# A Griffin / RWKV-7 trunk: half of the FFN's gate and up blocks by seven products of halves

## The chip, the cores and the metric

The kernel runs on one core of a Trainium2 chip. The metric is the time of one execution on the device in microseconds; the median of three runs before the change is 1319.34 us (1317.73 to 1319.41).

## What is computed

The input is 512 tokens of 1024 features, float32. Two layers follow each other: an RG-LRU block and an FFN, then an RWKV-7 block and an FFN, then a norm. The change touches the FFN, which each layer has once:

```python
def _conv_ffn(x, norm, w_up, conv_w, conv_b, w_down):
    h = _rmsnorm(x, norm)
    u = jnp.einsum('btd,df->btf', h, w_up)
    gate = _causal_dwconv(u[..., :D_FF], conv_w, conv_b)
    hid = jax.nn.gelu(gate, approximate=True) * u[..., D_FF:]
    return jnp.einsum('btf,fd->btd', hid, w_down)
```

D_FF is 3072, the convolution has three taps along the tokens, and `x + _conv_ffn(x)` goes on to the next block.

## The kernel before

Activations lie transposed: features on the 128 partitions, the 512 tokens along a row. x is eight such blocks (KB = 8). Every product of float32 is made of three matmuls on float32r parts (`mm3`, lines 51 to 53): high x high, high x low, low x high. So a block of a weight matrix (128 x 128) costs three matmuls of 512 columns. Weights come from HBM as raw tiles of 128 x 1024 floats (512 KB), on SP's queue, in the order of a written plan (`plan_weights`); ACT rounds each to its high part (line 90), DVE subtracts for the low part (line 93). Raw tiles and parts share one ring of 21 slots of 4 KB a partition (`b4`) with the eight pairs of parts of the normed input (`xs`), which stay in it as long as gate and up products need them.

An FFN has 24 gate blocks and 24 up blocks of 128 features. `gate_up` makes a third of them: four gate blocks, four up blocks, and again. `project` takes four blocks at once, over raw tiles of two blocks of the sum by four blocks of output, with four PSUM banks of eight. The norm's root isn't in xs: it comes as a row `rb` that multiplies each result (lines 581 and 592) and is itself made while the first matmuls run (`norm_end`: a sum over partitions on PE, a power on POOL at line 307, a broadcast on PE, a copy on ACT). A gate block then goes through the convolution (ACT line 584, DVE line 586 twice) and the gelu (ACT line 588); an up block is multiplied by rb and by the gelu (lines 592 and 593) and split into parts `hid`. `down` takes a third of the hidden blocks (eight) through w_down and adds to x (line 637) in the first FFN; in the second it works with hid as the stationary operand, so that the result stands by tokens, and adds to `xtok` (line 630), which `by_tokens` has made from x by transposes. The order is: third 0, third 1, down 0, third 2, down 1, down 2.

The framework that builds the queues of the engines keeps roughly to the order of the program, moves instructions by its own planned times, gives out the slots and sets the waits; on the chip each queue runs in order. Weights are asked for three tiles and split two tiles ahead of their use (`next_weights`). Work of other stages is handed out in small steps between the matmuls (`push`, `background`).

Before the first FFN `fin` (line 532) makes x and its parts while the last product of the RG-LRU block runs; before the second the one at line 1444 does so. After the first FFN, `spill` makes the parts for the RWKV-7 block, in tiles that the FFN no longer needs; at the end `finish` (line 1485 on) squares, norms and stores the output.

## Time and profile before

| | us |
|---|---|
| median of three runs | 1319.34 |
| profiled execution, its own time | 1318.34 |
| its span | 1316.6 |
| PE busy | 1296.2 (98%) |
| PE's weight loads busy | 1057.5 (80%) |
| DVE busy | 842.1 (64%) |
| ACT busy | 609.2 (46%) |
| POOL busy | 72.5 (6%) |
| mean granted clock of PE | 0.998 |

Shares are of the span. PE's matmuls overlap one another in the record, so that a matmul's duration there is longer than the distance to the next one's start. In rows that group instructions stand the line, the engine, the operation, the output and inputs with their shapes, how often, and then the total busy time in us and the mean of one in ns; behind the second bar is the idle time of the engine before them and what ended it. Rows of the timeline begin with the start and the duration in us.

### The profile page before, as it was taken

The page shows a single profiled execution, that of the slowest core. Times are in us where ns is not written, and L with a number is a line of the kernel's source. Part 1 is how long each engine was busy: PE and PEld are TensorE (multiplying, and loading weights), DVE is VectorE, ACT ScalarE, POOL GpSimd, SP SyncE. Part 2 cuts the span into 40 slices and gives each one's busy share as a digit, 9 for nine tenths or more (in the row PEclk, how much of TensorE's full clock was granted, in tenths as well). Part 3 has the DMA queues.
Part 4 walks back from the last instruction along what each step waited for, and adds up shares of the span by engine and source line. Part 5 has one row for each costly group of instructions (what it writes and reads, how often), then busy time and mean ns, then how long its engine had stood idle before and what let it go on. Part 6 is the DMA issues. An engine that isn't in the chain of part 4 may idle for free.

```text
span 1316.6 us, 20618 instructions
## 1 busy us (share of the span) xinstructions
PE 1296.2 (98%) x8547; PEld 1057.5 (80%) x8547; DVE 842.1 (64%) x1276; ACT 609.2 (46%) x964; POOL 72.5 (6%) x114
## 2 busy tenths in 40 slices
PE   9999999999999999999999999999999999999998
PEld 7877888888888888876678787778888888888886
DVE  5988756555436555587989975777564554365523
ACT  6897544233224423358844567655542332244311
POOL 4000000000000000021001121210000000000000
PEclk9999999999999999999999999999999999999999
DMA  6323333323233443213303112133333222334311
GB/s 194 116 64 97 96 112 96 96 64 96 97 96 96 128 116 109 95 37 95 108 25 97 43 53 83 43 97 96 97 96 96 64 96 96 96 96 128 113 63 64
DMA packets 72126, 120.30 MB, mean 91 GB/s; under 512 B 9498, under 2 KB 21476, under 8 KB 71904
## 3 DMA queue, kind: packets, MB, share of 16 engines
q1 hardware_dynamic: 70672, 117.20, 28.6%
q8 instruction: 67, 1.10, 0.3%
q10 hardware_dynamic: 576, 1.05, 0.2%
q0 software_dynamic: 784, 0.74, 0.2%
q14 instruction: 27, 0.22, 0.1%
HBM read 114.44 MB, written 4.52 MB: 90 GB/s over the span
## 4 chain that ended last, share of the span: by engine, by line
PE 85%; DVE 8%; ACT 5%; issue 1%; DMA 0%; SPq 0%; POOLq 0%; POOL 0%; DVEq 0%; ACTq 0%
PE acc L51 22%; PE acc L53 22%; PE acc L52 21%; PE acc L626 3%; PE acc L625 3%; PE acc L627 3%; DVE X L1053 1%; DVE wl L93 1%; DVE DA L1051 1%; PE s L1171 1%; ACT L483 1%; PE pd L1253 1%; ACT L472 0%; PE py L1264 0%; PE pe L1215 0%
## 5 line engine op out<-in xcount | busy, mean ns | idle before, releaser
L51 PE MATMUL acc<-xs,wh 128*128 128x512 f32 x896 | 350.2, 392 | 0.3 <-ACT wh L90 0.3
L53 PE MATMUL acc<-xs,wl 128*128 128x512 f32 x896 | 348.3, 390 | 1.4 <-DVE wl L93 1.4
L93 DVE TENSOR_TENSOR wl<-raw,wh 128x1024 fp32r<-128x1024 f32 (+1 forms) x201 | 242.8, 1216 | 166.1 <-PE acc L52 94.8
L52 PE MATMUL acc<-xs,wh 128*128 128x512 f32 x896 | 348.8, 389 | 0.0
L90 ACT CAST wh<-raw 128x1024 fp32r<-128x1024 f32 (+1 forms) x201 | 207.9, 1045 | 259.2 <-DVE wl L93 169.8
L53 PEld LDWEIGHTS acc<-xs,wl 128*128 128x128 f32 x896 | 168.2, 188 | 37.7 <-DVE wl L93 2.2
L51 PEld LDWEIGHTS acc<-xs,wh 128*128 128x128 f32 x896 | 168.1, 188 | 35.4 <-ACT wh L90 0.8
L52 PEld LDWEIGHTS acc<-xs,wh 128*128 128x128 f32 x896 | 168.3, 188 | 34.4
L586 DVE SCALAR_TENSOR_TENSOR cv<-gpad,pv,cv 128x512 f32<-128x512 f32 x96 | 71.9, 749 | 22.1 <-ACT cv L584 21.0
L90 ACT CAST hid<-un 128x512 fp32r<-128x512 f32 x48 | 29.8, 620 | 108.6 <-DVE un L593 108.6
L626 PE MATMUL acc<-wh,hid 128*128 128x512 f32 (+1 forms) x200 | 76.8, 384 | 0.0
L625 PE MATMUL acc<-wh,hid 128*128 128x512 f32 (+1 forms) x200 | 76.5, 382 | 0.0
L627 PE MATMUL acc<-wl,hid 128*128 128x512 f32 (+1 forms) x200 | 75.9, 380 | 0.0
L52 PE MATMUL acc<-hid,wh 128*128 128x512 f32 x192 | 75.7, 394 | 0.0
L53 PE MATMUL acc<-hid,wl 128*128 128x512 f32 x192 | 75.6, 394 | 0.0
L51 PE MATMUL acc<-hid,wh 128*128 128x512 f32 x192 | 75.5, 393 | 0.0
L592 DVE TENSOR_TENSOR un<-acc,rb 128x512 f32<-128x512 f32 x48 | 33.1, 689 | 44.3 <-PE acc L53 44.3
L93 DVE TENSOR_TENSOR hid<-un,hid 128x512 fp32r<-128x512 f32 x48 | 33.2, 691 | 31.1 <-ACT hid L90 31.1
L584 ACT ACTIVATE cv<-gpad,pv 128x512 f32<-128x512 f32 x48 | 39.2, 817 | 20.7 <-DVE gpad L581 20.5
L588 ACT ACTIVATE ge<-cv 128x512 f32<-128x512 f32 x48 | 30.1, 627 | 35.9 <-DVE cv L586 35.9
L630 DVE TENSOR_TENSOR xtok<-xtok,acc 128x512 f32<-128x512 f32 (+1 forms) x25 | 16.6, 666 | 45.5 <-PE acc L627 45.5
L625 PEld LDWEIGHTS acc<-wh,hid 128*128 128x128 f32 x200 | 37.5, 188 | 8.0
(424 smaller groups left out, 2165.8 us busy)
## 6 DMA issues: line engine op xcount, KB each, us to landing
raw<-in_ffn_w_up_dram SPq DMA_DIRECT2D x96, 512.0 KB, 3.8
raw<-in_ffn_w_down_dram SPq DMA_DIRECT2D x48, 512.0 KB, 3.7
raw<-in_rwkv_w_rkv_dram SPq DMA_DIRECT2D x24, 512.0 KB, 3.9
raw<-in_lru_w_in_dram SPq DMA_DIRECT2D x16, 512.0 KB, 3.9
raw<-in_lru_w_out_dram SPq DMA_DIRECT2D x8, 512.0 KB, 3.9
raw<-in_rwkv_w_out_dram SPq DMA_DIRECT2D x8, 512.0 KB, 3.6
xd<-x SPq DMA_DIRECT2D x8, 256.0 KB, 2.0
AR<-xd SPq DMA_DIRECT2D x1, 2048.0 KB, 7.9
```

Of the source, the lines that this page charges most:

```text
L51: nc.tensor.matmul(ps, wh, xh, start=start, stop=False)
L52: nc.tensor.matmul(ps, wh, xl, start=False, stop=False)
L53: nc.tensor.matmul(ps, wl, xh, start=False, stop=stop)
L90: put = (self.nc.vector.tensor_copy if dve else self.nc.scalar.copy)(hi, src)
L93: self.nc.vector.tensor_tensor(lo, src, hi.bitcast(F32), ALU.subtract)
L584: nc.scalar.activation(cv, gp[:, 0:T], AF.Identity, bias=self.vec(f"ffn_conv_b{l}", fb), scale=cw(0))
L586: nc.vector.scalar_tensor_tensor(cv, gp[:, j : j + T], cw(j), cv, ALU.mult, ALU.add)
L588: nc.scalar.activation(ges[o], cv, AF.Gelu_apprx_tanh)
L592: nc.vector.tensor_tensor(un, ps, rbs[0], ALU.mult)
L625: nc.tensor.matmul(ps, hh[:, s], wh[:, k, m], start=kk == 0, stop=False)
L626: nc.tensor.matmul(ps, hl[:, s], wh[:, k, m], start=False, stop=False)
L627: nc.tensor.matmul(ps, hh[:, s], wl[:, k, m], start=False, stop=kk == 7)
```

## The change

The gate and up blocks are taken in twelve pairs an FFN: two gate and two up blocks of the same features. Even pairs (`Whole`) are made as before, but in four products of half a sum each (G0, U0, G1, U1; the digit is the half of the eight blocks of the sum), every product 24 matmuls of 512 columns. Odd pairs (`Halves`) are made by Winograd's form of Strassen's scheme. The two output halves are up and gate, the two halves of the sum are blocks 0 to 3 and 4 to 7, and the columns are halved into tokens 0 to 255 and 256 to 511; seven products of halves take the place of eight. A product is 24 matmuls of 256 columns. Its weight operand is one of four raw tiles or one of three further sums of them, which POOL makes (four additions, one of them in place), split into parts like a raw tile; its moving operand is a half of xs or one of four sums of halves, which `operands` makes once an FFN on DVE and ACT and keeps as parts in tiles named xt. Products 1, 6, 7 and 4 add up in one bank, 5 and 3 in a second, 2 stands alone; ACT copies the first bank away after 1, 6 and 7, and DVE combines the copies with the other banks.

The products of all pairs stand in one list (`seq`); weights are split two products ahead of the one being emitted (`ahead`), and the first pairs overlap in it (one product of pair 2 lies between the fifth and sixth of pair 1). `down` comes after the odd pairs, for four hidden blocks at a time and eight at the end, and the last two products of a Halves pair are issued within it. Its additions to x or xtok double. In the second FFN the up results aren't multiplied by rb any more; the root is a third operand of the additions to xtok. The hidden tiles of half the pairs take x's place there, and the tiles for the RWKV-7 block's parts and the load of the last norm's gain vector (a DMA on POOL's queue) take the place of the sums xt. The raw tiles of the gate and up weights have four blocks of the sum by 256 columns instead of two by 512.

```diff
@@ -108,23 +110,26 @@
-            def dd(third):
+            def gu(six):
+                for i in range(2):
+                    c = six * 512 + i * 256
+                    self.quads.append(len(plan))
+                    for half, r in ((i, 0), (1 - i, 0), (0, 512), (1, 512)):
+                        add(up, r, half * DFF + c, 4, True)
+            def dd(row, n):
                 for g in range(2):
-                    for k in range(0, 8, 2):
-                        add(dn, third * 1024 + k * P, g * 512)
+                    for k in range(0, n, 2):
+                        add(dn, row + k * P, g * 512)
             gu(0)
-            gu(1)
-            dd(0)
-            gu(2)
-            dd(1)
-            dd(2)
+            for six in range(1, 6):
+                gu(six)
+                if six < 5:
+                    dd((six - 1) * 512, 4)
+            dd(2048, 8)
...
+    def norm_part(self, b, gain):
+        hi, lo = self.norm_block(b, gain)
+        if b >= KB // 2:
+            return hi, lo
+        nc, xb, H = self.nc, self.x[:, b, :], T // 2
+        if b % 2 == 0:
+            self.halves = self.b4(F32, (2, 2, H), f"xd{b}")
+        d = self.halves[:, b % 2]
+        nc.scalar.mul(d[:, 0], xb[:, H:], gain)
+        nc.vector.scalar_tensor_tensor(d[:, 1], xb[:, 0:H], gain, d[:, 0], ALU.mult, ALU.subtract)
+        return hi, lo, d[:, 0], d[:, 1]
...
-            def gate_up(third):
-                hid = []
...
-                            hh, hl = hx[:, 0], hx[:, 1]
-                        self.split(un, hh, hl)
...
+            H = T // 2
+            two = lambda ps: ps.rearrange("p (e t) -> p e t", e=2)
+            sums = [pool.tile([P, 2, 4, H], F32R, tag="xt", name="xt", bufs=4) for _ in range(4)]
+            gain = lambda b: self.vec("ffn_norm", l * 8 + b)
+            def operands():
+                n1, t2, t3, t4 = sums
+                def parts(t, k, f):
+                    nc.scalar.copy(t[:, 0, k], f)
+                    nc.vector.tensor_tensor(t[:, 1, k], f, t[:, 0, k].bitcast(F32), ALU.subtract)
+                for k in range(4):
+                    parts(n1, k, xs[k][3])
+                stt, f = nc.vector.scalar_tensor_tensor, {}
+                for k in range(4):
+                    xb = self.x[:, 4 + k, :]
+                    f[k] = two(t("s", 7))
+                    t2f, t4f = f[k][:, 0], f[k][:, 1]
+                    stt(t2f, xb[:, H:], gain(4 + k), xs[k][3], ALU.mult, ALU.add)
+                    parts(t2, k, t2f)
+                    stt(t4f, xb[:, 0:H], gain(4 + k), t2f, ALU.mult, ALU.subtract)
+                for k in range(4):
+                    if k % 2 == 0:
+                        t3f = two(t("s", 7))
+                    stt(t3f[:, k % 2], self.x[:, 4 + k, H:], gain(4 + k), xs[k][2], ALU.mult, ALU.subtract)
+                    parts(t3, k, t3f[:, k % 2])
+                for k in range(4):
+                    parts(t4, k, f[k][:, 1])
+                op = {i: [tuple(part[:, h] for part in xs[k + k0][:2]) for k in range(4)]
+                      for i, k0, h in ((1, 0, slice(0, H)), (2, 4, slice(0, H)), (3, 4, slice(H, T)))}
+                for i, v in ((5, n1), (6, t2), (7, t3), (4, t4)):
+                    op[i] = [(v[:, 0, k], v[:, 1, k]) for k in range(4)]
+                return op
+            op = {}
...
+            rb = lambda u, v: rbs[0][:, u:v].unsqueeze(1).to_broadcast([P, 2, v - u])
+            tt, gt = nc.vector.tensor_tensor, nc.gpsimd.tensor_tensor
+            class Pair:
+                def __init__(pair, n):
+                    i = quads[n]
+                    self.weights_load(i + 4)
+                    pair.n, pair.gp = n, gpads[n % 2]
+                    raws = [self.loaded.pop(i + j) for j in range(4)]
+                    pair.f = dict(zip(pair.names, raws))
+                    pair.w, pair.bank, pair.s = {}, {}, {}
+                def parts(pair, p):
+                    f = pair.f[p]
+                    hi, lo = self.b4(F32R, (4, 256), f"hi{p}"), self.b4(F32R, (4, 256), f"lo{p}")
+                    nc.scalar.copy(hi, f)
+                    tt(lo, f, hi.bitcast(F32), ALU.subtract)
+                    pair.w[p] = hi, lo
...
+            class Whole(Pair):
+                names = ("G0", "U0", "G1", "U1")
+                order = (names,)
+                def weights(pair, p):
+                    pair.parts(p)
+                def product(pair, p):
+                    hi, lo = pair.w.pop(p)
+                    k0 = int(p[1]) * 4
+                    for e in range(2):
+                        if not k0:
+                            pair.bank[p[0], e] = self.bank("acc" + p[0])
+                        ps = pair.bank[p[0], e]
+                        for k in range(4):
+                            c = slice(e * P, e * P + P)
+                            self.mm3(ps, (hi[:, k, c], lo[:, k, c]), xs[k0 + k][:2], k0 + k == 0, k0 + k == 7)
+                        if p == "G1":
+                            tt(pair.gp[:, e, 2:], ps, rbs[0], ALU.mult)
+                            pair.gate(e)
+                        if p == "U1":
+                            if not e:
+                                pair.room()
+                            un = t("s", 7)
+                            tt(un, ps, pair.ge[:, e] if last else rbs[0], ALU.mult)
+                            if not last:
+                                tt(un, un, pair.ge[:, e], ALU.mult)
+                            self.split(un, pair.hid[:, e, 0], pair.hid[:, e, 1])
+                        self.background(1)
+            class Halves(Pair):
+                names = (1, 7, 4, 2)
+                order = ((1, 5, 6, 2, 7), (4, 3))
+                def weights(pair, p):
+                    f = pair.f
+                    if p == 1:
+                        f[5], f[6], f[3] = (self.b4(F32, (4, 256), name) for name in ("S1", "S2", "S4"))
+                        gt(f[5], f[7], f[4], ALU.add)
+                        gt(f[6], f[5], f[1], ALU.subtract)
+                        gt(f[7], f[1], f[7], ALU.subtract)
+                        gt(f[3], f[6], f[2], ALU.subtract)
+                    pair.parts(p)
+                def product(pair, p):
+                    name = {1: "A", 5: "F", 2: "D"}.get(p)
+                    if name:
+                        pair.bank[name] = two(self.bank("acc" + name))
+                    ps = pair.bank[name or {3: "F"}.get(p, "A")]
+                    hi, lo = pair.w.pop(p)
+                    for e in range(2):
+                        c = slice(e * P, e * P + P)
+                        for k in range(4):
+                            self.mm3(ps[:, e], (hi[:, k, c], lo[:, k, c]), op[p][k], bool(name) and e + k == 0, e + k == 4, more=not name)
+                        self.background(0.5)
+                    s, bank, gp = pair.s, pair.bank, pair.gp
+                    lo, hi = slice(0, H), slice(H, T)
+                    if p in (1, 6, 7):
+                        s[p] = two(t("s", 7))
+                        nc.scalar.copy(s[p], bank["A"])
+                    if p == 2:
+                        tt(s[1], s[1], bank["D"], ALU.add)
+                        if not last:
+                            tt(s[1], s[1], rb(0, H), ALU.mult)
+                    if p == 7:
+                        tt(s[7], s[7], bank["F"], ALU.subtract)
+                        tt(gp[:, :, 2 + H :], s[7], rb(H, T), ALU.mult)
+                    if p == 4:
+                        tt(gp[:, :, 2 : 2 + H], bank["A"], rb(0, H), ALU.mult)
+                        for e in range(2):
+                            pair.gate(e)
+                    if p == 3:
+                        tt(s[6], s[6], bank["F"], ALU.subtract)
+                        if not last:
+                            tt(s[6], s[6], rb(H, T), ALU.mult)
+                        pair.room()
+                        for x, h in ((s[1], lo), (s[6], hi)):
+                            tt(x, x, pair.ge[:, :, h], ALU.mult)
+                            nc.scalar.copy(pair.hid[:, :, 0, h], x)
+                            tt(pair.hid[:, :, 1, h], x, pair.hid[:, :, 0, h].bitcast(F32), ALU.subtract)
+            quads = self.quads[l * 12 : l * 12 + 12]
+            pairs, hids = {}, []
+            W, S = Whole.names, Halves.order
+            seq = [(0, p) for p in W] + [(1, p) for p in S[0]] + [(2, W[0])] + [(1, p) for p in S[1]] + [(2, p) for p in W[1:]]
+            for n in range(3, 12, 2):
+                seq += [(n, p) for p in S[0] + S[1]]
+                if n < 11:
+                    seq += [(n + 1, p) for p in W]
+            made, at = [0], [0]
+            def ahead(j):
+                while made[0] < min(j, len(seq)):
+                    n, p = seq[made[0]]
+                    if n not in pairs:
+                        pairs[n] = (Halves if n % 2 else Whole)(n)
+                    pairs[n].weights(p)
+                    made[0] += 1
+            def products(upto, more=2):
+                while True:
+                    n, p = seq[at[0]]
+                    at[0] += 1
+                    ahead(at[0] + more)
+                    pairs[n].product(p)
+                    if p in ("G0", 1):
+                        self.weights_load(quads[n] + (8 if n + 1 < 12 and quads[n + 1] == quads[n] + 4 else 6))
+                    if n == 0 and p in ("G0", "U0"):
+                        start(int(p == "U0"))
+                        if p == "U0":
+                            op.update(operands())
+                    if p == 7:
+                        self.weights_split(quads[n] + 6)
+                    if (n, p) == upto:
+                        return
+            def down(n, b0, blocks, between, then):
+                final = n == 11
+                pieces = blocks // 2
                 for g in range(2):
                     if last:
                         pss = [self.bank(f"acc{o}") for o in range(4)]
                         end = final and g == 1
-                        for cs in [range(4)] if end else [(0,), (1,), (2, 3)]:
+                        for cs in [range(pieces)] if g else [(i,) for i in range(pieces)]:
...
-                                    if cs[-1] == 3:
-                                        n = slice(g * 512 + m.start, g * 512 + m.stop)
-                                        nc.vector.tensor_tensor(xtok[:, b, n], xtok[:, b, n], ps, ALU.add)
+                                            nc.tensor.matmul(ps, hh[:, s], wl[:, k, m], start=False, stop=kk == blocks - 1)
+                                    if cs[-1] == pieces - 1:
+                                        m = slice(g * 512 + m.start, g * 512 + m.stop)
+                                        nc.vector.scalar_tensor_tensor(xtok[:, b, m], ps, self.rs[:, b : b + 1], xtok[:, b, m], ALU.mult, ALU.add)
                                         if final:
-                                            finish(b, n, xtok[:, b, :], pool)
+                                            finish(b, m, xtok[:, b, :], pool)
+                            if not g and cs[0] == 0:
+                                between()
+                        if not g:
+                            then()
...
+            rooms = []
+            def room(b):
+                if b % 2 == 0:
+                    rooms.append(pool.tile([P, 2, 2, T], F32R, tag="xt", name="hx", bufs=4))
+                return rooms[-1][:, b % 2, 0], rooms[-1][:, b % 2, 1]
+            for n in range(3, 12, 2):
+                products((n, 7))
+                if n == 11 and not last:
+                    self.norm_begin()
+                    self.push(self.lora_weights())
+                down(n, 2 * n - 6, 4 if n < 11 else 8, lambda: products((n, 3)), lambda: ahead(at[0] + 2))
             if not last:
                 after()
...
             nc.vector.tensor_tensor(self.x[:, b, :], xr[:, b, :], ps, ALU.add)
-            xs[b] = self.norm_block(b, self.vec("ffn_norm", 8 + b))
+            xs[b] = self.norm_part(b, self.vec("ffn_norm", 8 + b))
...
+        def spill(b, room):
             nc.sync.dma_start(self.xd[:, b, :], self.x[:, b, :])
-            if b < 4:
-                w = t("hid", 12, F32R, 2 * T)
-                room = w[:, 0:T], w[:, T:]
-            else:
-                tag, n = (("ge", 5), ("ge", 5), ("cv", 2), ("un", 2))[b - 4]
-                room = t(tag, n, F32R), t(tag, n, F32R)
-            hs.append(self.norm_block(b, self.vec("rwkv_norm", b), room))
+            hs.append(self.norm_block(b, self.vec("rwkv_norm", b), room(b)))
         self.ffn(0, xs, spill, lambda: self.rwkv_lora(hs))
...
             if not fgs:
-                fgs.append(pool.tile([P, D], F32, name="fg"))
+                fgs.append(pool.tile([P, 2, D], F32, tag="xt", name="fg", bufs=4)[:, 0])
```

More of the change, by code (lines that the diff above doesn't have):

```diff
@@ L547, in ffn @@
             rbs, norm = [], []
-            gpads = [pool.tile([P, T + 2], F32, name=f"gpad{i}") for i in range(2)]
+            gpads = [pool.tile([P, 2, T + 2], F32, name=f"gpad{i}") for i in range(2)]
             for u in gpads:
-                nc.vector.memset(u[:, 0:2], 0.0)
+                nc.vector.memset(u[:, :, 0:2], 0.0)
+            late = []
             xtok = None
@@ new lines, in ffn, with hidden @@
+            op = {}
+            def hidden(n):
+                if last and n // 2 % 2:
+                    if n == 2:
+                        self.drain()
+                    if n % 2 == 0:
+                        self.xhid = self.const.tile([P, 2, 2, 2, T], F32R, tag="x", name="hid", bufs=1)
+                    return self.xhid[:, n % 2]
+                return pool.tile([P, 2, 2, T], F32R, tag="hid", name="hid", bufs=2 if last else 4)
+            rb = lambda u, v: rbs[0][:, u:v].unsqueeze(1).to_broadcast([P, 2, v - u])
```

104 lines of the change are left out of this document (44 added, 60 removed).

## Prediction

> **What bounds the kernel now.** I read the profile's page first (span, busy shares, chain), then the stages, then the rows of single matmuls.
>
> ```profile
> span 1316.6 us, 20618 instructions
> PE 1296.2 (98%) x8547; PEld 1057.5 (80%) x8547; DVE 842.1 (64%) x1276; ACT 609.2 (46%) x964; POOL 72.5 (6%) x114
> PE 85%; DVE 8%; ACT 5%; issue 1%; DMA 0%; SPq 0%; POOLq 0%; POOL 0%; DVEq 0%; ACTq 0%
> ...
> 100.00:158.50 58.50, 58.18 (x256) 47.52 (x255) 45.12 (x60) 34.82 (x49) 0.00 (x0) 1.00 0.29 91
> 180.00:400.00 220.00, 220.00 (x966) 180.98 (x965) 116.58 (x145) 72.64 (x88) 0.00 (x0) 1.00 0.29 91
> 950.00:1200.00 250.00, 250.00 (x1102) 206.68 (x1102) 134.23 (x167) 83.42 (x101) 0.00 (x0) 1.00 0.29 91
> ```
>
> The last three rows are stages: length, then busy time of PE, PEld, DVE, ACT and POOL, granted clock, DMA share, GB/s. Inside both FFNs PE is busy for the whole stage at clock 1.00 while DVE is busy 53% of it (116.58 of 220; 134.23 of 250), ACT 33%, DMA 29%. So an FFN lasts as long as its matmuls, at the rate at which they start. PE's busy time overlaps itself, so the rate comes from start times, in the timeline:
>
> ```profile
> 199.74 0.39 PE L52 MATMUL acc<-xs,wh 128*128 128x512 f32 x1
> ...
> 205.86 0.39 PE L52 MATMUL acc<-xs,wh 128*128 128x512 f32 x1
> ...
> 550.39 0.39 PE L51 MATMUL acc<-hid,wh 128*128 128x512 f32 x1
> ...
> 555.06 0.39 PE L53 MATMUL acc<-hid,wl 128*128 128x512 f32 x1
> ...
> 777.57 0.28 PE L1001 MATMUL acc<-wl,mix 128*128 128x256 f32 x1
> ...
> 779.96 0.28 PE L1000 MATMUL acc<-wh,mix 128*128 128x256 f32 x1
> ...
> 1304.50 0.28 PE L625 MATMUL acc<-wh,hid 128*128 128x256 f32 x1
> ...
> 1310.04 0.28 PE L627 MATMUL acc<-wl,hid 128*128 128x256 f32 x1
> ```
>
> There are 27 starts from the first of these rows to the second: 6.12 / 27 = 226.7 ns for 512 columns with xs as moving operand. The next pair spans 20 starts: 4.67 / 20 = 233.5 ns when the moving operand is hid, a tile of the FFN's own pool. For 256 columns: 2.39 / 20 = 119.5 ns in the v projection, 5.54 / 47 = 117.9 ns in the last product. The page's 0.28 and 0.39 us are latencies and not the price.
>
> **PE's gain.** A pair (two gate and two up blocks) takes 4 blocks x 8 k x 3 parts = 96 matmuls of 512: 96 x 0.2267 = 21.76 us. As halves it takes 7 products x 2 x 4 x 3 = 168 of 256 columns. Two halves cost more than one whole (2 x 117.9 = 235.8 against 226.7), so the eighth that is saved in columns, 2.7 us, isn't all kept. No row shows a 256-column matmul on the tiles named xt, in the FFN's pool, where four products (5, 6, 7, 4) have their moving operand; the other three read xs. Bounds: 117.9 for all seven gives 168 x 0.1179 = 19.81 us, a gain of 1.96 a pair; hid's whole excess of 6.8 ns on the four gives (3 x 117.9 + 4 x 124.7) / 7 = 121.8, or 20.46 us and 1.30 a pair. I take half the excess, since a matmul of half the length is nearer to half of it: (3 x 117.9 + 4 x 121.3) / 7 = 119.8 ns, beside the v projection's 119.5: 20.13 us, 1.63 a pair. Twelve pairs: **19.6 us less** (15.6 to 23.5). Against it, in the first FFN four hidden blocks that lay in the b4 ring move to the FFN's pool, and their 4 x 8 x 3 = 96 matmuls with them to the slower 233.5: +0.7.
>
> [...]
>
> **What DVE and ACT get for it.** Prices by form:
>
> ```profile
> L93 DVE TENSOR_TENSOR wl<-raw,wh 128x1024 fp32r<-128x1024 f32 x199 | 241.5, 1221 | 165.1 <-PE acc L52 94.8 <-ACT wh L90 47.5 <-PE acc L626 14.0
> L586 DVE SCALAR_TENSOR_TENSOR cv<-gpad,pv,cv 128x512 f32<-128x512 f32 x96 | 71.9, 749 | 22.1 <-ACT cv L584 21.0
> L592 DVE TENSOR_TENSOR un<-acc,rb 128x512 f32<-128x512 f32 x48 | 33.1, 689 | 44.3 <-PE acc L53 44.3
> L630 DVE TENSOR_TENSOR xtok<-xtok,acc 128x512 f32<-128x512 f32 x23 | 15.8, 687 | 45.1 <-PE acc L627 45.1
> L90 ACT CAST wh<-raw 128x1024 fp32r<-128x1024 f32 x199 | 206.8, 1049 | 258.1 <-DVE wl L93 169.8 <-DMA raw<-in_ffn_w_down_dram 30.9 <-PE acc L52 17.1
> L1133 ACT COPY x<-acc 128x512 f32<-128x512 f32 x8 | 4.7, 586 | 2.1 <-PE acc L1001 2.0
> L364 ACT ACTIVATE sqin<-xin 128x256 f32<-128x256 f32 x16 | 6.4, 421 | 0.0
> 1310.35 0.42 DVE L630 TENSOR_TENSOR xtok<-xtok,acc 128x256 f32<-128x256 f32 x1 [0.42 <-PE acc L627]
> ```
>
> A whole pair keeps four weight splits (4 x 1.22), gate work (2 x (0.69 + 2 x 0.75)) and up work (2 x 3 x 0.69): 13.4 us of DVE. A halves pair has seven splits (8.5), about nine 512-wide combinations (6.2, and 1.4 more for the root in the first FFN) and the convolution (3.0): 19.1. A sixth down has four splits and eight additions: 4.9 + 5.5 = 10.4. One round of halves, whole and sixth: 42.9 us of DVE in 20.1 + 21.8 + 21.8 = 63.7 us of PE, 67% instead of 53%; ACT similarly 26 us. Both fit on average. The doubled additions of the sixths (16 x 0.69 = 11 us an FFN) lie under matmuls; with that cover gone they would cost up to 11 an FFN. The last root moved into the additions takes 24 multiplications of 0.69 off DVE in the second FFN and turns each token addition into a three-operand one (0.75 beside 0.69): on the path only at the very end, +0.03 us. Both are off PE: 0.
>
> **The weight sums on POOL.** Four 128x1024 additions a halves pair, 48 in all. POOL has no such row; the nearest:
>
> ```profile
> L1285 POOL TENSOR_TENSOR bv<-x,bon 128x512 f32<-128x512 f32 x8 | 8.7, 1084 | 23.8 <-DVE BK L93 9.5 <-DVE var L1286 8.8 <-PE bont L1327 5.5
> L1280 DVE SCALAR_TENSOR_TENSOR ytok<-mu,ytok 128x512 f32<-128x512 f32 x8 | 6.2, 777 | 0.3
> 763.18 1.04 POOL L1285 TENSOR_TENSOR bv<-x,bon 128x512 f32<-128x512 f32 x1
> 763.40 1.37 DVE L1280 SCALAR_TENSOR_TENSOR ytok<-mu,ytok 128x512 f32<-128x512 f32 x1
> 840.99 0.68 DVE L1292 TENSOR_TENSOR ytok<-ytok,lnw 128x512 f32<-128x512 f32 x1
> 841.21 1.37 POOL L1285 TENSOR_TENSOR bv<-x,bon 128x512 f32<-128x512 f32 x1 [3.10 <-DVE BK L93]
> ```
>
> Twice 1.08 makes 2.17 us an addition (2.74 if each is held up as at 841.21), 8.7 us a pair. They start when the four raw tiles have landed and b4 slots are free, which is at the latest when the whole pair before begins its third product, 10.9 us ahead of the first halves product; the first sum is wanted by the second product, the next by the third. That lies beside PE. But the rows show the two engines holding each other up: L1280 took 1.37 us under POOL's addition where its group's mean is 0.777, and POOL took 1.37 after starting under L1292 where it otherwise took 1.04. So POOL's 8.7 us may come on top of DVE's 42.9: 51.6 of 63.7, 81%. In the tight stretch, from 10.9 us before a halves pair to the end of its fifth product (14.4 us in), DVE has seven splits, gate and up work of the pair before and 1.4 of combination, 18.4 us, or 27.1 with POOL's hold, in 25.3. The excess of 1.8 is less than the two products (5.8 us) by which splits run ahead. I take 0 here, bounds 0 to 1.8.
>
> [...]
>
> **Accumulators read between products.** ACT must copy bank A after product 1 before product 6 may add to it, with product 5 (24 x 0.12 = 2.9 us) between. The copy is 0.59; two weight casts queued ahead of it make 2.7 us, three 3.7. So 0 to 0.8 a pair; behind it on ACT wait the casts of the next products. I take 0.3 for ten pairs: **+3** (0 to 26, with this 0.8 and the 1.8 above in every one).
>
> **The start of each FFN.** The sums of xs are made there: 16 subtractions and 12 three-operand sums of 128x256, each near 0.42, are 11.8 us of DVE and 16 casts (6.7) of ACT.
>
> ```profile
> 158.19 0.39 PE L51 MATMUL acc<-xs,wh 128*128 128x512 f32 x1
> 160.93 0.68 DVE L291 TENSOR_TENSOR sqacc<-sqacc,sq 128x512 f32<-128x512 f32 x1
> ```
>
> From the first matmul at 158.19 to the third halves product there are 4 x 5.44 + 2 x 2.88 = 27.5 us. DVE owes in them: the norm's end (to 161.6, some 2.9 busy), six splits (7.3), the sums (11.8), pair 0's gate (4.4) and up work (4.1): 30.5, so 3.0 too much, 11.7 with all of POOL's hold. Before it DVE had 13.4 us idle in 58.5 (45.12 busy), where sums of the first four blocks can go, and up work can wait. Bounds 0 to 11.7; I take 3.0, twice: **+6**. The norm's four extra differences (0.42 each on DVE and ACT) lie in that idle time.
>
> **Moved and reordered.** The weights are the same bytes in as many loads, with rows of 1 KB for 2 KB; some loads of the v projection have that shape already:
>
> ```profile
> raw<-in_ffn_w_up_dram SPq DMA_DIRECT2D x96, 512.0 KB, 3.8
> raw<-in_rwkv_w_rkv_dram SPq DMA_DIRECT2D x24, 512.0 KB, 3.9
> ```
>
> Landing costs the same (3.9 beside 3.8). A halves pair's seven splits, three sums and the next raw tiles want 12 to 13 of the 13 ring slots that xs leaves, so on SP a load can wait for a slot, and every later load behind it; a quad is asked for at least a whole product (5.4 us) before its first cast, against 3.8 of landing: 0, and up to 3.8 at a pair whose load is that late. The gain vector's load goes from the start of the second FFN behind the last sums on POOL, some 30 us before its use: 0. The second FFN's hidden tiles in x's place wait for its transposes, issued 40 us earlier: 0.
>
> **Sum.** -19.6 + 0.7 + 3 + 6 = -9.9 us. On the profiled execution (1318.34 us, 1.74 of it around the span) this gives 1308.4; the median of the runs, 1319.34, is 1.00 higher, so **1309**.
>
> **Rivals.** (a) *Nothing stalls*: the queues cover sums and copies, and PE keeps 19 to 23.5 us: 1296 to 1300. For it: DVE idles 47% now. Against it: the shortfall at the FFN's start. (b) *The lock reaches PE*: POOL's sums hold DVE's splits, casts wait for sums at the head of ACT's queue, and the lookahead of two short products (5.8 us, where whole ones gave 10.9) runs out. It decides from 19.6 / 12 = 1.6 us a pair on; with a third of the 8.7 on the path, 2.9 x 12 = 35, it ends near 1335. For it: the two overlaps; against it: 5.8 us of cover. [...] (c) *The starts eat it*: DVE short by 8 at each FFN's start, 16 + 3 + 0.7 against 19.6: 1319.
>
> **Chances.** Forecast 0.46, (a) 0.26, (b) 0.15, (c) 0.13. A difference under 0.2% (2.6 us) can't be told from none here. Faster: all of (a) and all but 0.02 of the forecast, 0.70; same: 0.02 and most of (c), 0.10; slower: (b) and the rest of (c), rounded up, 0.20. The likeliest case alone is 1302 to 1316. The range, 1297 to 1324, takes in most of (a) and all of (c) and leaves out (b)'s greater part.
>
> **What would show it.** Starts of 256-column matmuls 117.9 to 121.8 ns apart in the halves; POOL rows of 128x1024 near 2.2 us, and subtractions of 1.22 us stretched beside them; PE without gaps in the middle of an FFN and idle by about 3 us in the first halves pair of each; FFN stages some 5 us shorter each (the first lasts 397 now, from 158.19 to just after 555.06). Wrong if PE waits in every halves pair, if halves start over 125 ns apart, or if DVE is busy above 85% of an FFN.

## The result, and the profile after

The changed kernel takes **1334.84 us** (median of 4 runs, 1333.41 to 1335.48) against 1319.34: a ratio of 1.0119, 95% interval 1.0101 to 1.0136. It is slower by 15.5 us where 10 us less were forecast. Three lines of the page of the changed kernel (span, busy time, granted clock by slice):

```profile
span 1333.0 us, 22694 instructions
PE 1287.4 (97%) x9411; PEld 1086.1 (81%) x9411; DVE 966.3 (72%) x1420; ACT 668.9 (50%) x1076; POOL 189.1 (14%) x162
...
PEclk9999998999999999999999999999999999999999
```

The mean granted clock over the span is 0.987, where it was 0.998 before. The stages say where that happened. The first fence is of before, the second of after; columns: stretch, length, busy time of PE, PEld, DVE, ACT, POOL, granted clock, DMA share, GB/s.

```profile
158.00:275.00 117.00, 117.00 (x526) 97.11 (x525) 71.69 (x95) 47.93 (x59) 1.94 (x1) 1.00 0.32 99
275.00:400.00 125.00, 125.00 (x547) 102.33 (x546) 59.20 (x72) 35.33 (x42) 0.00 (x0) 1.00 0.28 89
```

```profile
158.00:275.00 117.00, 103.05 (x586) 91.19 (x585) 92.89 (x110) 51.54 (x75) 23.11 (x9) 0.93 0.28 90
275.00:400.00 125.00, 125.00 (x711) 109.10 (x711) 79.62 (x98) 46.88 (x59) 19.09 (x8) 1.00 0.32 102
...
162.66:169.40 6.74, 6.43 (x15) 4.61 (x16) 6.74 (x14) 2.96 (x5) 0.00 (x0) 0.51 0.51 138
...
200.60:207.40 6.80, 6.80 (x34) 6.80 (x35) 3.85 (x4) 4.15 (x5) 0.00 (x0) 0.54 0.32 110
```

In the middle of the FFN (275 to 400) PE never waits, its clock is whole, and DVE is busy 64% of the time: there the change does what it should. In the first 117 us PE idles for 14 us, and twice it then runs at about half clock, for 6.7 and 6.8 us.

**PE's gain is larger than forecast.** Starts of single matmuls in a halves pair in the middle of the FFN (timeline of after; start, latency, engine, line, tiles):

```profile
435.29 0.39 PE L51 MATMUL accU<-xs,loU 128*128 128x512 f32 x1
...
438.01 0.39 PE L51 MATMUL accU<-xs,loU 128*128 128x512 f32 x1
...
438.47 0.28 PE L51 MATMUL accA<-xs,lo 128*128 128x256 f32 x1
...
440.99 0.28 PE L51 MATMUL accA<-xs,lo 128*128 128x256 f32 x1
...
441.35 0.28 PE L51 MATMUL accF<-xt,lo 128*128 128x256 f32 x1
...
446.45 0.28 PE L51 MATMUL accA<-xt,lo 128*128 128x256 f32 x1
```

The row with lo is every third matmul. So 512 columns of xs take 2.72 / 12 = 226.7 ns, 256 of xs 2.52 / 21 = 120.0, and 256 of xt 5.10 / 45 = 113.3. A halves pair is 72 x 0.1200 + 96 x 0.1133 = 19.52 us against 21.76: 2.24 less, 26.9 for twelve. The span grew by 16.4, so 26.9 + 16.4 = **43.3 us were lost elsewhere**.

**Where they went.** The groups of after on PE that waited longest (count | busy, mean ns | idle before, what ended it), then a POOL and a DVE group:

```profile
L51 PE MATMUL accG<-xs,hiG 128*128 128x512 f32 x384 | 122.2, 400 | 7.8 <-ACT hiG L673 7.8
L51 PE MATMUL accA<-xt,hi 128*128 128x256 f32 x576 | 104.7, 284 | 10.6 <-ACT s L752 10.6
...
L51 PE MATMUL accF<-xt,lo 128*128 128x256 f32 x96 | 27.6, 287 | 4.4 <-DVE lo L674 4.4
...
L731 POOL TENSOR_TENSOR S<-raw,raw 128x1024 f32<-128x1024 f32 x12 | 32.2, 2685 | 507.7 <-DMA raw<-in_ffn_w_up_dram 385.1 <-PE accF L51 71.7 <-DVE loU L674 50.5
L685 DVE SCALAR_TENSOR_TENSOR cv<-gpad,pv,cv 128x512 f32<-128x512 f32 x96 | 86.0, 926 | 14.2 <-ACT cv L683 13.8
```

The waits are 7.8 + 10.6 + 4.4 = 22.8 us. The clock costs 0.013 x 1333.0 = 17.3 where it cost 0.002 x 1316.6 = 2.6: 14.7 more. Not all of that lies behind these waits. The row of 158 to 275 above has 0.07 x 117 = 8.2 of it, and three stretches of the second FFN 1.7 + 0.5 + 1.2 = 3.4:

```profile
926.00:960.00 34.00, 29.61 (x148) 24.50 (x147) 32.00 (x48) 17.31 (x32) 13.03 (x5) 0.95 0.21 63
960.00:1010.00 50.00, 46.93 (x304) 42.66 (x303) 38.81 (x37) 24.30 (x34) 10.93 (x4) 0.99 0.27 85
1010.00:1040.00 30.00, 28.25 (x184) 25.78 (x183) 21.73 (x27) 17.52 (x23) 0.00 (x0) 0.96 0.43 141
```

The rest of the half clock is in the RWKV-7 block (0.53 and 0.54 for 3.40 us each, from 661.00 and 801.00) and after the last matmul (0.50 from 1330.00 to 1333.00). So the waits and the clock behind them are 22.8 + 11.6 = 34.4 of the 43.3 us; for the other 8.9 no cause is shown. Some 2 of them lie in the RWKV-7 block between the FFNs (555.3 to 911.4 before, 568.0 to 926.2 after). The 22.8 us of waits lie in two places of each FFN. The first is its start; the columns are those of the timeline, with the idle time before and what ended it in brackets:

```profile
158.84 0.39 PE L51 MATMUL acc<-out,wl 128*128 128x512 f32 x1
...
161.58 1.03 ACT L673 CAST hiG<-raw 128x1024 fp32r<-128x1024 f32 x1
...
162.66 1.65 PE L51 MATMUL accG<-xs,hiG 128*128 128x512 f32 x3 [3.44 <-ACT hiG L673]
```

Before, the first product followed the last matmul of the stage at once, since its weights had been split while that stage ran. In the changed kernel the splits of gate and up blocks are made by the pair itself, two products ahead of their use, and for the first product nothing is ahead: its cast begins 2.7 us after the last matmul of the stage has begun. The second FFN waits 4.38 us in the same place.

The second place is halves pairs 1 and 3 (the first two). Pair 1 of the first FFN, POOL, DVE, ACT and PE of after:

```profile
174.49 3.52 POOL L731 TENSOR_TENSOR S<-raw,raw 128x1024 f32<-128x1024 f32 x1 [0.47 <-DVE s L635]
175.66 5.16 DVE L635 SCALAR_TENSOR_TENSOR s<-x,pv,xd 128x256 f32<-128x256 f32 x2
...
180.74 6.50 DVE L620 TENSOR_TENSOR xt<-s,xt 128x256 fp32r<-128x256 f32 x6
...
183.04 2.58 POOL L734 TENSOR_TENSOR S<-S,raw 128x1024 f32<-128x1024 f32 x1
...
198.71 0.69 DVE L718 TENSOR_TENSOR s<-s,ge 128x512 f32<-128x512 f32 x1
...
199.43 0.62 ACT L91 CAST hid<-s 128x512 fp32r<-128x512 f32 x1 [1.36 <-DVE s L718]
...
199.95 0.58 ACT L752 COPY s<-accA 128x512 f32<-128x512 f32 x1
...
200.58 0.80 PE L51 MATMUL accA<-xt,hi 128*128 128x256 f32 x2 [4.21 <-ACT s L752]
```

Read from the bottom: PE waits 4.21 us for ACT's copy of bank A, which could have been made at the end of product 1, some 7 us earlier. But ACT takes the cast of pair 0's hidden block first (199.43), which waits 1.36 us for DVE's L718, and the copy behind it (199.95). The weight sums themselves aren't late: POOL ends the first at 178.0, and ACT casts it at 188.5 only, when it has waited 5.77 us for a subtraction on DVE. DVE is late because of the top: while POOL makes its four sums (174.5 to 185.6), DVE gets eight small instructions of the sums of xs done in 5.16 + 6.50 = 11.7 us, which take 2 x 0.48 + 6 x 0.42 = 3.5 undisturbed. Pair 3 shows the same, with pair 1's convolutions in place of the sums of xs:

```profile
223.19 2.60 POOL L731 TENSOR_TENSOR S<-raw,raw 128x1024 f32<-128x1024 f32 x1 [37.58 <-PE accF L51]
...
223.45 11.30 DVE L685 SCALAR_TENSOR_TENSOR cv<-gpad,pv,cv 128x512 f32<-128x512 f32 x4
...
244.61 0.39 PE L51 MATMUL accF<-xt,lo 128*128 128x256 f32 x1 [1.93 <-DVE lo L674]
...
251.03 0.69 PE L51 MATMUL accA<-xt,hi 128*128 128x256 f32 x2 [3.63 <-ACT s L752]
```

Four L685 take 11.30 us instead of 4 x 0.75 = 3.0: about one DVE instruction for each of POOL's, which in turn go from 2.40 to 2.6 and 2.85. In the second FFN the waits are shorter: 1.04 us in pair 1, 2.03 and 1.75 in pair 3. In the later halves pairs the burst meets next to nothing. Pair 7, after:

```profile
416.22 0.39 PE L51 MATMUL acc<-hid,wl 128*128 128x512 f32 x1
...
419.83 2.40 POOL L731 TENSOR_TENSOR S<-raw,raw 128x1024 f32<-128x1024 f32 x1 [54.46 <-DMA raw<-in_ffn_w_up_dram]
...
428.42 2.19 DVE L674 TENSOR_TENSOR lo<-raw,hi 128x1024 fp32r<-128x1024 f32 x1 [9.64 <-ACT hi L673]
```

There a sixth of the products down has just ended, the convolutions are done under it, and DVE is idle for 9.64 us; one subtraction is held, 2.19 instead of 1.22.

### The profile page after: what moved, and what is told of

It reads as the page before. It is cut to its first block, busy times and chain, and to the rows that moved or that the text cites. A ratio compares the mean times of both kernels' runs of the same rounds, so it can differ in the third digit from the quotient of the medians.

```text
span 1333.0 us, 22694 instructions
## 1 busy us (share of the span) xinstructions
PE 1287.4 (97%) x9411; PEld 1086.1 (81%) x9411; DVE 966.3 (72%) x1420; ACT 668.9 (50%) x1076; POOL 189.1 (14%) x162
## 5 line engine op out<-in xcount | busy, mean ns | idle before, releaser
L94 DVE TENSOR_TENSOR wl<-raw,wh 128x1024 fp32r<-128x1024 f32 (+1 forms) x105 | 126.2, 1208 | 21.0 <-ACT wh L91 16.8
L51 PE MATMUL accG<-xs,hiG 128*128 128x512 f32 x384 | 122.2, 400 | 7.8 <-ACT hiG L673 7.8
L91 ACT CAST wh<-raw 128x1024 fp32r<-128x1024 f32 (+1 forms) x105 | 108.0, 1037 | 23.9 <-DMA raw<-in_ffn_w_down_dram 5.4
L51 PE MATMUL accU<-xs,hiU 128*128 128x512 f32 x384 | 118.7, 390 | 0.0
L51 PE MATMUL accA<-xt,hi 128*128 128x256 f32 x576 | 104.7, 284 | 10.6 <-ACT s L752 10.6
L51 PEld LDWEIGHTS accA<-xt,hi 128*128 128x128 f32 x576 | 91.1, 195 | 12.6 <-ACT s L752 11.6
L685 DVE SCALAR_TENSOR_TENSOR cv<-gpad,pv,cv 128x512 f32<-128x512 f32 x96 | 86.0, 926 | 14.2 <-ACT cv L683 13.8
L51 PE MATMUL accA<-xt,lo 128*128 128x256 f32 x288 | 81.5, 283 | 0.0
L51 PE MATMUL acc<-xs,wh 128*128 128x512 f32 x256 | 80.2, 394 | 0.5 <-ACT wh L91 0.5
L51 PE MATMUL accG<-xs,loG 128*128 128x512 f32 x192 | 76.3, 398 | 0.3 <-DVE loG L674 0.3
L51 PE MATMUL accU<-xs,loU 128*128 128x512 f32 x192 | 74.8, 389 | 0.0
```

The costliest lines, as they stand in the source:

```text
L51: mm = lambda *a, **kw: self.nc.tensor.matmul(ps, *a, skip_group_check=more, **kw)
L91: put = (self.nc.vector.tensor_copy if dve else self.nc.scalar.copy)(hi, src)
L94: self.nc.vector.tensor_tensor(lo, src, hi.bitcast(F32), ALU.subtract)
L685: nc.vector.scalar_tensor_tensor(cv, pair.gp[:, e, j : j + T], cw(j), cv, ALU.mult, ALU.add)
```

## The experiments

Theory: the loss lies in the two starts (first product not split ahead) and in DVE being held under POOL's sums in pairs 1 and 3, each with the half clock behind its waits. Rivals: too much DVE work at the start whoever holds it; the halves as such; the place of tiles in SBUF.

**1. Split the first gate block ahead again.**

```diff
-            if self.plan[i][2]:
+            if self.plan[i][2] and i not in (self.quads[0], self.quads[12]):
...
-                    raws = [self.loaded.pop(i + j) for j in range(4)]
+                    raws = [self.loaded.pop(i + j, None) for j in range(4)]
...
                 def parts(pair, p):
                     f = pair.f[p]
+                    if f is None:
+                        pair.w[p] = self.splitted.pop(quads[pair.n])
+                        return
```

> The changed kernel, with the first raw tile of each FFN (G0 of pair 0) split into its parts during the stage before, as the kernel before did. Theory S (the FFN's start loses the time: nothing is split ahead, then DVE owes more than it can do): the two gaps of 3.8 and 4.8 us ahead of the first matmul go, and with them part of the stretches at half clock behind them (6.8 and 3.4 us long, worth half of that); 1322 to 1329 us. Rival L (POOL's hold of DVE in every halves pair is the whole loss): the gaps are paid elsewhere, 1332 to 1335.

Measured: 1323.08 us, ratio to the kernel before 1.0027 (1.0018 to 1.0037), so 11.8 less than the changed kernel. Groups of this kernel on PE:

```profile
L51 PE MATMUL accG<-xs,hiG 128*128 128x512 f32 x352 | 108.8, 390 | 0.0
...
L51 PE MATMUL accA<-xt,hi 128*128 128x256 f32 x576 | 102.4, 280 | 7.9 <-ACT s L755 7.9
```

The waits of the first products are gone (7.8 to 0.0), those of pairs 1 and 3 have mostly stayed (10.6 to 7.9); pair 0 waits anew, 1.88 and 0.96 us for splits on DVE. 11.8 us come back for 7.8 of waiting: less of the time is at half clock, too (the mean clock is 0.992 instead of 0.987).

**2. No sums on POOL.** The three tiles S are set to zero on POOL and the fourth sum is left out.

```diff
-                        gt(f[5], f[7], f[4], ALU.add)
-                        gt(f[6], f[5], f[1], ALU.subtract)
-                        gt(f[7], f[1], f[7], ALU.subtract)
-                        gt(f[3], f[6], f[2], ALU.subtract)
+                        nc.gpsimd.memset(f[5], 0.0)
+                        nc.gpsimd.memset(f[6], 0.0)
+                        nc.gpsimd.memset(f[3], 0.0)
```

> The changed kernel without the sums of weights: POOL fills the three new tiles with zeros, which reads no SBUF, and the fourth addition is left out, so the results of the halves pairs are not the reference's; slots, splits and matmuls stay. Theory S with the hold as its part: DVE isn't held 8.6 us in pairs 1 and 3 of each FFN; their stalls (5.0, 5.9, 1.2 and 4.3 us) and the half clock behind them go, the gaps at the start stay; 1313 to 1321 us. Rival L (every pair pays): 1300 or less. Rival X (the sums of xs alone overload DVE): 1328 or more.

Measured: 1312.18 us, ratio 0.9943 (0.9927 to 0.996), 22.7 less than the changed kernel. Its groups on PE and DVE:

```profile
L51 PE MATMUL accG<-xs,hiG 128*128 128x512 f32 x384 | 122.0, 400 | 7.9 <-ACT hiG L673 7.9
L51 PE MATMUL accA<-xt,hi 128*128 128x256 f32 x576 | 100.5, 277 | 0.0
...
L685 DVE SCALAR_TENSOR_TENSOR cv<-gpad,pv,cv 128x512 f32<-128x512 f32 x96 | 68.8, 748 | 11.2 <-ACT cv L683 10.7
```

The start's wait stays, the waits in pairs 1 and 3 are gone, and L685 is back from 926 to 748 ns. DVE's own work is the same as in the changed kernel, so it isn't the work but the hold.

**3. No sums of xs.** The operand sums n1 are used in all four places; twelve subtractions, twelve three-operand sums and twelve casts an FFN are left out (the lines that make t2, t3 and t4 go with them).

```diff
-                for i, v in ((5, n1), (6, t2), (7, t3), (4, t4)):
+                for i, v in ((5, n1), (6, n1), (7, n1), (4, n1)):
```

> The changed kernel without three of the four sums of xs: products 5, 6, 7 and 4 all use the first, so 12 subtractions, 12 three-operand sums and 12 casts an FFN are left out and the results are not the reference's. Theory S: pair 1's stall (5.0 and 1.2 us) shrinks or goes, pair 3's (5.9 and 4.3 us) stays for the most part, since POOL's hold of 8.6 us remains there; 1322 to 1330 us. Rival X (these sums are the overload): pair 3's goes as well, 1312 to 1318.

Measured: 1326.92 us, ratio 1.0053 (1.0038 to 1.0068). Timeline of this kernel, DVE and PE in pair 3:

```profile
215.16 11.30 DVE L670 SCALAR_TENSOR_TENSOR cv<-gpad,pv,cv 128x512 f32<-128x512 f32 x4
...
236.33 0.39 PE L51 MATMUL accF<-xt,lo 128*128 128x256 f32 x1 [1.93 <-DVE lo L659]
...
242.75 0.80 PE L51 MATMUL accA<-xt,hi 128*128 128x256 f32 x2 [2.58 <-ACT s L737]
```

Pair 1 has no wait any more: POOL's burst there meets little of DVE's. Pair 3 is held as before, 11.30 us for the same four convolutions. So the backlog of the start is not what stalls pair 3. Leaving out this work brings 7.9 us, a third of what leaving out POOL's sums brings.

**4. Pair 1 whole.** Five halves pairs an FFN for six; pair 1's blocks by full products.

```diff
-                    for half, r in ((i, 0), (1 - i, 0), (0, 512), (1, 512)):
+                    h = i if six else 0
+                    for half, r in ((h, 0), (1 - h, 0), (0, 512), (1, 512)):
...
-            seq = [(0, p) for p in W] + [(1, p) for p in S[0]] + [(2, W[0])] + [(1, p) for p in S[1]] + [(2, p) for p in W[1:]]
+            seq = [(n, p) for n in range(3) for p in W]
...
-                        pairs[n] = (Halves if n % 2 else Whole)(n)
+                        pairs[n] = (Halves if n % 2 and n > 1 else Whole)(n)
```

> The changed kernel with pair 1 of each FFN whole, so five halves pairs instead of six; the result stays the reference's. It gives up 2 x 2.2 us of PE's gain. Theory S: DVE has 22 us more for the sums of xs and no hold in them; pair 1's stall goes and pair 3's too, since DVE is no longer behind when its hold comes; 1318 to 1325 us. Rival L (a hold beside DVE work in any pair): pair 3 now stalls as pair 1 did, 1332 to 1340.

Measured: 1317.84 us, ratio 0.9987 (0.9977 to 0.9997), 17.0 less than the changed kernel although 2 x 2.24 = 4.5 us of PE's gain are given back. Timeline of this kernel, POOL and DVE ahead of pair 3:

```profile
214.51 2.78 POOL L732 TENSOR_TENSOR S<-raw,raw 128x1024 f32<-128x1024 f32 x1 [40.31 <-DVE loU L675]
...
215.72 2.11 DVE L94 TENSOR_TENSOR hid<-s,hid 128x512 fp32r<-128x512 f32 x1 [0.69 <-ACT hid L91]
...
223.75 2.26 DVE L675 TENSOR_TENSOR lo<-raw,hi 128x1024 fp32r<-128x1024 f32 x1 [5.91 <-ACT hi L674]
```

Pair 3 is still made of halves with its sums on POOL, but with pair 1 whole no convolution falls into the burst, DVE idles 5.91 us in it, and PE doesn't wait there. What is held matters, not that something overlaps.

**5. The sums of pairs 1 and 3 on DVE.**

```diff
                     if p == 1:
+                        gt = nc.vector.tensor_tensor if pair.n < 4 else nc.gpsimd.tensor_tensor
```

> The changed kernel with the four sums of weights of pairs 1 and 3 made on DVE; POOL makes those of the other pairs as before. Theory S with the hold as its part: DVE pays 4 x 1.22 = 4.9 us for itself where POOL's run kept it for 8.6, and the runs that remain lie where DVE has next to nothing to do; the stalls in pairs 1 and 3 shrink by about 3.7 us each and with them some half clock, 1322 to 1330 us. If the hold isn't the cause but the DVE work as such, 4.9 us more of it makes each stall longer: 1338 or more.

Measured: 1310.64 us, ratio 0.9947 (0.9925 to 0.9968), 24.2 less than the changed kernel and more than I had expected. Its five runs spread from 1308.37 to 1315.97, so the gain is known to a few microseconds. Groups of this kernel:

```profile
L51 PE MATMUL accA<-xt,hi 128*128 128x256 f32 x576 | 100.5, 277 | 0.0
...
L733 DVE TENSOR_TENSOR S<-S,raw 128x1024 f32<-128x1024 f32 x4 | 4.9, 1220 | 0.1
```

Four sums cost DVE 4 x 1.22 = 4.9 us; on POOL they held it for over 8. DVE has more to do at the start than in the changed kernel, and in pairs 1 and 3 nothing waits: the rival of too much work, whoever holds DVE, doesn't explain these waits. The first product still waits 3.44 and 4.40 us in this kernel, which gives DVE that time; experiment 8 shows what is left when it doesn't.

**6. Two repairs that leave the sums on POOL: edits 1 and 4 together.**

> Both cures of the first series: G0 split during the stage before, and pair 1 of each FFN whole (five halves pairs); the result stays the reference's. Theory S: the two gains add, since one lies ahead of the first matmul and the other in pairs 1 and 3: 1319.6 - 2 - 11 gives 1304 to 1310 us. If both took away the same loss, 1316 to 1319.

Measured: 1302.87 us, ratio 0.9883 (0.9865 to 0.9901). Less than the changed kernel by 32.0, where the two alone give 11.8 + 17.0 = 28.8: separate causes. The 3.2 us more are within the spread of this kernel's runs (1301.32 to 1306.04).

**7. Do addresses set the rate of the matmuls?** The kernel before, and the kernel of experiment 6, each with 32 more bytes in the constant pool, which moves every later tile.

```diff
         self.pv = c.tile([P, 4 * P], F32, name="pv")
+        c.tile([P, 8], F32, name="pad")
```

> The kernel before, with 32 bytes more in the pool of constants, so that every tile behind them (weights, xs, hidden) begins 32 bytes later in its partition, at a multiple of 64; nothing else changes. Theory A (where the moving operand begins sets the rate of matmuls: 226.7 ns at 512 columns for xs, 233.5 for hid, and at 256 columns 120 for halves of xs but 113.5 for xt): rates change, likely towards 216 to 227 for all, 1270 to 1315 us. Rival (the tile's own content or the pair of operands sets it): 1318 to 1321.

> The kernel with both cures and the 32 bytes more in the pool of constants; the result stays the reference's. Theory A: the same rates for every operand, and the gain of the kernel before with the 32 bytes on top of the cures' gain. Rival: as the kernel with both cures alone, within 2 us.

Measured: 1319.23 us, ratio 0.9997 (0.9988 to 1.0007), and 1300.84 us, ratio 0.9866 (0.985 to 0.9883; without the shift 0.9883, and the intervals overlap). The matmuls don't change with the shift: their mean durations are 392, 389 and 390 ns from xs and 393 to 394 from hid in the kernel before and in the shifted one, 391 from xs and 277 from xt (each with the weights' high parts) in experiment 6's kernel and in its shifted one. No run shows the 216 ns for 512 columns that the theory's range goes down to: from xs and hid they took 226.7 and 233.5. The theory falls for this shift, the only one tried.

**8. All twelve halves pairs with both causes mended: edits 1 and 5 together.**

> The changed kernel with both repairs that keep all twelve halves pairs: the first gate block of each FFN is split during the stage before, and in pairs 1 and 3 of each FFN the weight sums are made on DVE instead of POOL. Theory (the loss is the two starts plus the hold of DVE under POOL's additions in pairs 1 and 3, and the two are separate): the gains found alone, 1334.8 - 1323.1 = 11.8 and 1334.8 - 1310.6 = 24.2, add up: 1298.9, range 1296 to 1303, with no stall over 1 us in the first 100 us of either FFN. Rival (with the first block split ahead, PE starts earlier against the same DVE work, and DVE falls short in pair 1): 1304 to 1312, with a stall of 2 us or more in pair 1.

Measured: 1300.5 us, ratio 0.9877 (0.986 to 0.9894), 34.3 less than the changed kernel; the sum of the two alone is 36.0. Two stretches of this kernel:

```profile
158.00:275.00 117.00, 114.24 (x669) 100.37 (x668) 94.53 (x134) 54.31 (x77) 4.94 (x3) 1.00 0.34 109
275.00:400.00 125.00, 125.00 (x711) 109.06 (x710) 82.16 (x100) 48.53 (x60) 16.67 (x8) 1.00 0.31 101
```

The clock is whole, and the first 117 us hold 669 matmuls where the changed kernel has 586. Part of the rival is there too: pair 1 of the first FFN still waits about 3 us in all, 1.62 of it at the head of product 2, because DVE now has the first products' work, the sums of xs and the weight sums in a row. With experiment 7's second kernel it is the fastest of the study; the two can't be told apart.

**9. Experiment 7's second kernel, with the sums of pair 3 on DVE.**

> The kernel with the first gate block split ahead, pair 1 whole and 32 spare bytes in the constant pool (1300.8), with the weight sums of pair 3 on DVE instead of POOL. Theory (POOL's hold costs only where the lookahead runs out; pair 3 showed no stall there, so nothing is to be had): 1300.8 within 1.5. Rival (additions on POOL cost PE something everywhere): 0.8 to 2.5 us less.

Measured: 1301.59 us, ratio 0.9871 (0.9855 to 0.9886), the same as without. Where PE has no wait, moving the sums from POOL to DVE brings nothing, as experiment 4's pair 3 had said.

## Why the prediction was wrong

**PE's gain** (19.6 us): right in kind, mis-sized. The halves on xs measured 120.0 ns, close to the v projection's 119.5 and above the 117.9 taken, but those on xt 113.3 instead of 121.3. The step was "hid's whole excess of 6.8 ns on the four", halved: that tiles of the FFN's pool share hid's slower rate. They don't, and the gain was 26.9. This error went the other way than the result.

**The start of each FFN** (6 us for both): the step that failed first. It counted "six splits" from the first matmul on and took PE's own start as given, since in the kernel before it is. That the first gate block's split moved with its pair from the stage before into the FFN follows from the `True` that the diff gives to `add`: tiles so marked aren't split ahead. It cost 11.8 us (experiment 1). The 3.0 us of DVE's shortfall, taken twice, came as waits of 2.8 in the first FFN and none in the second once start and hold were mended (experiment 8). Late by 3.44 and 4.38 us, PE then ran at about half clock (0.51 for 6.74 us, 0.54 for 3.40). The prediction asked what becomes late on DVE, and not whether the first product is ready.

**The weight sums on POOL** (0, bounds 0 to 1.8 a pair): the larger failure, 24.2 us (experiment 5). The 8.7 us of hold a pair, set down there as the worst case, came about where DVE had work: 11.7 - 3.5 = 8.2 and 11.3 - 3.0 = 8.3 in the rows above. Two things were wrong. The tight stretch was costed with an average halves pair's work, and so each pair got the same price; in fact PE waits in no product of the pairs 5 to 11, as a sixth down lies ahead of their burst, and the waits are all in pairs 1 and 3, as sums of xs or convolutions fall into it. No product down follows pair 1, so its convolutions (3.0 us) and the six instructions on its hidden blocks (4.1) come into pair 3's stretch, and the 18.4 us don't contain them. And "the two products (5.8 us) by which splits run ahead" were set against an excess of 1.8, where a hold of 8.2 or 8.3 is by itself longer than they are. In pair 3 DVE wasn't late before the burst: it had just been idle for 4.27 and 0.75 us. At the start the full hold stood in the bound (11.7) and not in the 3.0 taken.

**Accumulators read between products** (3 us): the wait came where it was named, at product 6 for the copy of bank A, and as a group it is PE's longest (10.6 us). But ahead of ACT's copy stand not the "two weight casts" but the hidden block's cast of the pair before, which waits for DVE. The cost is no term of its own: it is zero when DVE is on time (experiments 2, 4 and 5: 0.0 on accA).

**The half clock** was in no step. 11.6 of the 43.3 us are a lower granted clock behind waits. The windows at 162.66 and 200.60 show it: 0.51 and 0.54 for 6.7 and 6.8 us, behind waits of 3.44 and 4.21 us. So each of these two waits cost some 3 us more than its own length.

**The rivals.** Rival (b), POOL's hold of DVE reaching PE, gave 1335 and the time is 1334.84, but the agreement of the numbers is chance. It laid 2.9 us on each of twelve pairs; measured were on average some 6 us (24.2 / 4) on each of four, and the starts beside it. Of its two sides, "the two overlaps" was the right evidence, and "5.8 us of cover" the wrong one. Rival (c) had the right place, with DVE short by 8 as its price for each start, but the cause that it names (DVE's sum of work) is too small: with still more work on DVE, pairs 1 and 3 don't wait in experiment 5, and pair 1 of one FFN waits 2.8 us in experiment 8. The forecast's own sign stands only for the mended kernel: 1300.5, half a microsecond above rival (a)'s 1296 to 1300, with PE's larger gain of 26.9 less some 8 us that stay.

**What would show it**: FFN stages 5 us shorter were wrong (the first lasts 405 us from its first product, not under 397); PE idle by 3 us in the first halves pair was right in place, with 4.66 and 1.04 measured. None of the three signs of being wrong came, though the forecast was wrong: they looked for waits in every halves pair, a slower matmul, or a DVE busy all through the FFN (71% in the first, 289.5 of 410 us), and the loss lay in the first pairs.

## What to carry to other kernels

When work is moved from one helper to another, ask for its first use in each stage what used to prepare it ahead of the stage: averages over a stage hide the two or three places where the queue is empty. Price a hold between engines by what the held engine has to do in just those microseconds, pair by pair; the same 9.7 us of POOL additions cost nothing beside an idle DVE and some 6 us beside one with work, and doing them on the busy engine itself (4.9 us) was the cheaper way. And price a PE wait with the half clock that can follow it, here 3.4 to 6.8 us of it behind waits of 3.44 to 4.38.

## What the runs showed of the hardware

**Half clock behind waits.** Waits of 3.44 and 4.21 us were followed by 6.74 and 6.80 us at a mean clock of 0.51 and 0.54, those of 3.63 and 4.38 us by 3.40 us at 0.52 and 0.54 (from 251.00 and 930.70). Behind the wait of 1.93 us that ends at 244.61 the clock is 1.00 (244.60 to 248.00). One of 2.03 us, with no other wait in the 40 us before it, was followed by half clock, too (timeline of after):

```profile
1007.80 0.38 PE L51 MATMUL accF<-xt,lo 128*128 128x256 f32 x1 [2.03 <-DVE lo L674]
```

The stretch behind it, in the columns of the stages:

```profile
1010.00:1011.00 1.00, 1.00 (x7) 1.00 (x6) 1.00 (x2) 0.59 (x1) 0.00 (x0) 0.50 0.53 41
```

How long a wait must be for this is not shown.

**The rate of a matmul goes with the tile of its moving operand.** 256 columns take 120.0 ns from xs and 113.3 from xt, 512 take 226.7 from xs and 233.5 from hid. Experiments 2 (weight sums of zero) and 8 have the same 120.0 and 113.3 in pair 1, and with the tiles moved by 32 bytes (experiment 7) the mean durations stayed. The cause stays open.

**POOL's addition** of 128x1024 takes 2.40 us undisturbed, where twice its 128x512 row had given 2.17; DVE's takes 1.22.
